# Two heads, two scan outputs and two scan directions side by side on TensorE's columns, and one modulation vector of layer 0 computed during the output projection

## The chip, the cores and the metric

The kernel runs on one core of one Trainium2 chip. The metric is the device time of one execution in microseconds (us); less is better. A core has five engines with a queue each: PE (TensorE, the matmul array), DVE (VectorE), ACT (ScalarE), POOL (GpSimd) and SP (SyncE, which here only issues DMA transfers). Each queue runs in order, and the engines wait for one another by semaphores. Matmul results land in PSUM, 128 partitions wide; everything else is held in SBUF. A matmul keeps its stationary operand (`lhsT`, up to 128 × 128) in the array and streams the moving operand (`rhs`, up to 512 columns) past it; a stationary operand with 64 or 32 columns uses that many columns of the array, and its result that many PSUM partitions.

## The reference

A block of two layers over 512 latent tokens of width 1024, with 256 context tokens in front. Layer 0 projects the normalised tokens into attention heads and a state-space scan (SSD), runs both as parallel groups of heads, and joins them in one output projection; layer 1 is a gated short convolution; each layer ends in a SwiGLU FFN. What matters here is layer 0's mixer and the modulation:

```python
mod = (silu(c) @ ada_w[i] + ada_b[i])             # six vectors of 1024
sh1, sc1, g1, sh2, sc2, g2 = split(mod, 6)
hx = rms_norm(x, norm_mix[i]) * (1 + sc1) + sh1   # sc2, sh2 for the FFN
# attention: 8 query heads of 64, 2 key/value heads, 768 keys, 512 queries
s  = q @ keys.T * 64 ** -0.5
o  = softmax(s) @ vals
# scan: 8 heads of 64, chunks of 128 tokens, two directions f and b
y_diag = ((C @ B.T) * decay) @ (x * dt)           # inside a chunk
states = B.T @ (decay_to_end * x * dt)            # what a chunk hands on
y_off  = C @ (decay * h_in)                       # from the chunks before
y = y_f + y_b + d_skip * x
x = x + g1 * (concat(o, rms_norm(y * silu(z))) @ w_out)
x = x + g2 * swiglu(rms_norm(x) * (1 + sc2) + sh2)
```

## The kernel before

All tokens are kept transposed, features on partitions and tokens on columns. Large projections split both operands in two fp32r parts, `hi` and `lo`, and run three matmuls a tile (`mm3`, L116 to L118); the splits are one ACT cast and one DVE subtraction each (`split`, L94 and L95). A weight tile of 128 × 1024 comes by DMA into one of three buffers `wst`, and is split into `whi` and `wlo` (L94, L95); `take` keeps two weights loaded ahead.

Layer 0's mixer runs after the projections of k, v, dt and q. `heads_prep` normalises the heads and applies rotary position (`rope`, L552 on; queries are written twice, L565, so that a transposed head fills 128 partitions). The context scan (`ssd_context`) and the four last feature projections follow. Then three generators are stepped in turn, in one loop at the end of `mixer`: the scan (`ssd`: eight units, each one of four chunks and one of two groups of heads, `ssd_unit`), the attention (`attention`) and the modulation of layer 0 (`ada_rest` with parts 2, 3 and 4: the mixer's gate, and the FFN's shift and scale). The Tile framework then orders each engine's instructions by data and priority, so the order in the code is only a first hint; `order` rows below show what it made.

- `ssd_states` (L645): for one chunk and group, xw (POOL, L652) times the tokens of B, whose 64 columns are held twice so that the 128 rows of the result hold both directions; of a 128-row result one direction uses 64 rows.
- `ssd_unit` (L740): decay matrices through matmuls with triangular constants (L751 to L758), exponentials on ACT, the products with dt on DVE (L768 to L774), then `yp` (L779 and L780): for two heads at once, 128 stationary columns and 2 × 128 moving ones; of the result each head takes the half of the rows that is its own, in two DVE pieces on 64 partitions (L784).
- `attn_prep` (L787): the queries of a head by four PE transposes (L791), split into q1 and q2 (L795), a first pass over the scores that finds a common shift (L802 and L804), L808.
- `attn_head` (L811): three pairs of key chunks; for each, scores (L822) into a bank psS, the exponential on ACT (L824), then the values (L830): the stationary operand has 64 columns of values and 64 of ones (`vz`), so one matmul gives the head's output in 64 rows and the softmax's sums in the other 64. Two ACT copies (L843, L844) take them out. After each second head a DVE chain turns the sums into factors (L882 to L886) and applies them (L887).
- `ada_rest` (L236): per part two accumulators of 512 columns; each takes eight DVE products (one L255, seven L257), a transpose (L260) and a reduction (L261); all parts end in one small matmul with a constant (L264) and four additions (L269).

The output projection (`project`, L897, called in `run`) sits in a block in which PE's order is that of the code: 8 output tiles d over 8 input tiles k; for the first three tiles (lead) all k but attention's last (k = 3) come first, and k = 3 last; d = 3 and 4 are whole; the last three (tail) run in two token halves. After it the FFN's norm, FFN, short convolution and second FFN follow. PSUM has eight banks: psA three of 512 columns, psV one, psS two of 1024.

## Time and profile before

| | us |
|---|---|
| median of three runs | 1294.06 (1289.82 to 1294.98) |
| the profiled execution, whole | 1294.68 |
| its span in the trace | 1292.9 |
| PE busy | 1241.5 (96%) |
| DVE busy | 731.7 (57%) |
| ACT busy | 448.0 (35%) |
| POOL busy | 182.7 (14%) |
| mean granted clock of PE | 0.989 |

Times inside the trace count from the start of the span. Busy is time in which an engine has an instruction; ends of matmuls are modelled, so that the records of neighbouring matmuls overlap and the distance between two starts is what one costs. A matmul with fp32 operands leaves two records, with half of its passes each. The granted clock of a stretch is TensorE's: 1.00 is 2.4 GHz, 0.50 is 1.2 GHz. The scan and attention lie between 144 and 331 us, the output projection's matmuls between 316 and 366.

### The profile page before, as it was taken

How to read it: one execution, taken by the hardware profiler on the slowest of the kernel's cores; microseconds unless marked ns; L12 is line 12 of the kernel's file. 1: busy time of each engine (PE TensorE's matmuls, PEld its weight loads, DVE VectorE, ACT ScalarE, POOL GpSimd, SP SyncE). 2: the span in 40 equal slices, each digit the busy share in tenths (PEclk: the TensorE clock that was granted, in tenths of full speed). 3: DMA queues.
4: the chain of work that ended last, by engine and by line, in shares of the span. 5: the costliest groups of instructions: out<-in, count | busy, mean ns of one | idle time of the engine just before them, and what ended most of it. 6: DMA issues, size and time to landing. Idle time of an engine off the chain costs nothing.

```text
span 1292.9 us, 15877 instructions
## 1 busy us (share of the span) xinstructions
PE 1241.5 (96%) x6086; PEld 1022.4 (79%) x6086; DVE 731.7 (57%) x1187; ACT 448.0 (35%) x675; POOL 182.7 (14%) x199
## 2 busy tenths in 40 slices
PE   5999988899999999999999999999999999999997
PEld 3887665567798888888888988888988888888886
DVE  4898899976464777788522564443643333332223
ACT  4534534455353222222222342223532222222221
POOL 3433435440220000000000110002200000000001
PEclk9998989999999999999999999999999999999998
DMA  9331453300413777777433323333133333333322
GB/s 370 125 98 49 123 166 119 98 1 1 149 63 122 229 250 241 226 235 255 123 102 90 115 67 97 98 98 114 50 114 98 98 98 98 92 96 90 92 88 66
DMA packets 54845, 158.52 MB, mean 123 GB/s; under 512 B 6000, under 2 KB 8688, under 8 KB 54512
## 3 DMA queue, kind: packets, MB, share of 16 engines
q1 hardware_dynamic: 54480, 157.20, 38.3%
q8 instruction: 48, 0.79, 0.3%
q10 hardware_dynamic: 288, 0.31, 0.1%
q14 instruction: 29, 0.24, 0.1%
HBM read 154.86 MB, written 2.10 MB: 121 GB/s over the span
## 4 chain that ended last, share of the span: by engine, by line
PE 83%; DVE 9%; issue 3%; DMA 3%; POOL 1%; ACT 1%; SPq 0%; DVEq 0%; ACTq 0%; POOLq 0%
PE psS L116 14%; PE psS L117 14%; PE psS L118 14%; PE psA L116 10%; PE psA L118 10%; PE psA L117 10%; PE psV L830 2%; DMA adaw<-ada 2%; PE psS L961 1%; DVE xtok L257 1%; DVE mx L804 1%; PE psS L822 1%; DVE wlo L95 1%; PE psS L963 1%; DMA xT<-xT 1%
## 5 line engine op out<-in xcount | busy, mean ns | idle before, releaser
L95 DVE TENSOR_TENSOR wlo<-wst,whi 128x1024 fp32r<-128x1024 f32 (+2 forms) x194 | 234.9, 1214 | 317.2 <-ACT whi L94 311.8
L94 ACT CAST whi<-wst 128x1024 fp32r<-128x1024 f32 (+2 forms) x194 | 198.4, 1026 | 549.9 <-PE psS L117 258.5
L116 PE MATMUL psS<-act_hi,whi 128*128 128x512 f32 x760 | 297.5, 391 | 1.0 <-DVE cs_a L573 0.9
L118 PE MATMUL psS<-act_hi,wlo 128*128 128x512 f32 x760 | 297.2, 391 | 0.0
L117 PE MATMUL psS<-act_lo,whi 128*128 128x512 f32 x760 | 297.2, 391 | 0.0
L118 PEld LDWEIGHTS psS<-act_hi,wlo 128*128 128x128 f32 x760 | 143.3, 189 | 30.0
L116 PEld LDWEIGHTS psS<-act_hi,whi 128*128 128x128 f32 x760 | 143.2, 188 | 29.3 <-issue 1.2
L117 PEld LDWEIGHTS psS<-act_lo,whi 128*128 128x128 f32 x760 | 143.2, 188 | 27.7
L325 POOL TENSOR_TENSOR sq_acc<-sq_acc,sq 128x512 f32<-128x512 f32 (+1 forms) x28 | 38.0, 1356 | 872.2 <-issue 645.7
L116 PE MATMUL psA<-ffn_h_hi,whi 128*128 128x512 f32 (+1 forms) x396 | 145.4, 367 | 0.0
L117 PE MATMUL psA<-ffn_h_lo,whi 128*128 128x512 f32 (+1 forms) x396 | 145.0, 366 | 0.0
L118 PE MATMUL psA<-ffn_h_hi,wlo 128*128 128x512 f32 (+1 forms) x396 | 145.0, 366 | 0.0
L257 DVE SCALAR_TENSOR_TENSOR ada_acc<-ada_st,silu_c,ada_acc 128x512 f32<-128x512 f32 x98 | 73.5, 750 | 25.5 <-DMA ada_st<-ada 24.0
L117 PEld LDWEIGHTS psA<-ffn_h_lo,whi 128*128 128x128 f32 x396 | 74.7, 189 | 12.0
L118 PEld LDWEIGHTS psA<-ffn_h_hi,wlo 128*128 128x128 f32 x396 | 74.7, 189 | 12.1
L116 PEld LDWEIGHTS psA<-ffn_h_hi,whi 128*128 128x128 f32 x396 | 74.7, 189 | 11.9
L116 PE MATMUL psA<-act_hi,whi 128*128 128x512 f32 (+1 forms) x216 | 80.0, 370 | 0.1
L118 PE MATMUL psA<-act_hi,wlo 128*128 128x512 f32 (+1 forms) x216 | 79.2, 367 | 0.8 <-DVE wlo L95 0.8
L117 PE MATMUL psA<-act_lo,whi 128*128 128x512 f32 (+1 forms) x216 | 79.6, 368 | 0.0
L916 DVE SCALAR_TENSOR_TENSOR xT<-psA,mod,xT 128x512 f32<-128x512 f32 (+1 forms) x40 | 25.6, 643 | 67.9 <-PE psA L118 67.7
L94 ACT CAST ffn_h_hi<-sg 128x512 fp32r<-128x512 f32 x44 | 27.3, 621 | 59.0 <-DVE sg L980 59.0
L118 PEld LDWEIGHTS psA<-act_hi,wlo 128*128 128x128 f32 x216 | 40.8, 189 | 8.1 <-DVE wlo L95 1.3
(297 smaller groups left out, 1810.7 us busy)
## 6 DMA issues: line engine op xcount, KB each, us to landing
wst<-w_gu SPq DMA_DIRECT2D x88, 512.0 KB, 3.6
ada_st<-ada SPq DMA_DIRECT2D x112, 256.0 KB, 4.0
wst<-w_dn SPq DMA_DIRECT2D x32, 512.0 KB, 3.5
wst<-ada SPq DMA_DIRECT2D x24, 512.0 KB, 3.8
wst<-w_sc SPq DMA_DIRECT2D x24, 512.0 KB, 3.7
adaw<-ada SPq DMA_DIRECT2D x16, 512.0 KB, 10.4
wst<-w_dn SPq DMA_DIRECT2D x16, 384.0 KB, 3.2
wst<-w_f SPq DMA_DIRECT2D x10, 512.0 KB, 3.6
```

Of the source, the lines that this page charges most:

```text
L94: nc.scalar.copy(hi, src)
L95: nc.vector.tensor_tensor(lo, src, hi.bitcast(F32), ALU.subtract)
L116: nc.tensor.matmul(out, lhsT=a[0], rhs=b[0], start=start, stop=False)
L117: nc.tensor.matmul(out, lhsT=a[0], rhs=b[1], start=False, stop=False)
L118: nc.tensor.matmul(out, lhsT=a[1], rhs=b[0], start=False, stop=stop)
L257: nc.vector.scalar_tensor_tensor(a, w[:, i], c, a, ALU.mult, ALU.add)
L325: nc.gpsimd.tensor_tensor(self.acc[:, ts], self.acc[:, ts], sq, ALU.add)
L804: nc.vector.tensor_reduce(mx[:, c:c + 1], s[:, 0:768], AX.X, ALU.max)
L822: nc.tensor.matmul(s[:, a * T:a * T + T], lhsT=kt[x][:, ks], rhs=q[x], start=(x == 0), stop=(x == 1))
L830: nc.tensor.matmul(av, lhsT=vz[:, kc, vs], rhs=e[:, a], start=(c + a == 0), stop=(c + a == CHUNKS - 1))
L916: nc.vector.scalar_tensor_tensor(xt[:, d, ts], ps, gate[:, d:d + 1], xt[:, d, ts], ALU.mult, ALU.add)
L961: nc.tensor.matmul(out, lhsT=a[:, k * P:(k + 1) * P], rhs=hi, start=(k == 0 and a is w[0]), stop=False)
```

## The change

**Attention.** `attn_head` becomes `attn_pair`: two heads are worked on together. The values' stationary operand is 64 columns without the ones; head 0 goes to PSUM partitions 0 to 63, head 1 to 64 to 127. The softmax's sums come from matmuls of their own with 32 columns of ones, four of them in four column groups, into a bank psA that the pair holds (`sm`). One ACT copy of 128 partitions each takes out sums and outputs. After DVE's transpose of the sums a small matmul with a new constant `pair` (L894) adds the two parts of each head; the reciprocal reads PSUM. Exponentials and queries have four buffers each instead of two. `attn_prep` makes the queries by eight matmuls of 64 columns with the identity, in place of four transposes of 128, and `rope` writes queries once.

**Scan.** B's tokens are held once. `ssd_states` runs one matmul of 64 columns for each direction, in the two column halves; `yp` runs one for each head, and one DVE piece on 128 partitions (L783) reads both.

**Modulation.** Part 4 (the FFN's scale) leaves the mixer's loop. It is queued in front of the output projection and stepped there: twice after each lead tile, three times after d = 3 and 4, and to its end before the tail. Its 512 KB loads use the `wst` buffers of the weights.

```diff
-        vz = mp.tile([P, CHUNKS, 2, 192], F32, name="vz")
-        nc.gpsimd.memset(vz, 1.0)
+        vz = mp.tile([P, CHUNKS, 2, 64], F32, name="vz")
-        qd = mp.tile([P, 4, 8, 2, 64], F32, name="qd")
+        qd = mp.tile([P, 4, 8, 64], F32, name="qd")
...
-        ada = [self.ada_rest(None, 0, (2, 3, 4), (xtok[:, 0], xtok[:, 1]))]
+        ada = [self.ada_rest(None, 0, (2, 3), (xtok[:, 0], xtok[:, 1]))]
...
+            if len(dst.shape) == 3:
+                (nc.vector, nc.gpsimd)[i].tensor_tensor(dst[:, :, o:o + 32], u, v, op)
+                continue
             for e in range(2):
                 (nc.vector, nc.gpsimd)[e].tensor_tensor(dst[:, :, e, o:o + 32], u, v, op)
...
-            nc.tensor.matmul(st[:, lo:lo + n], lhsT=sd["btok"][:, c, g].rearrange("p a b -> p (a b)"),
-                             rhs=xw.rearrange("p a b c -> p (a b c)")[:, lo:lo + n], start=True, stop=True)
+            for c, e in ends:
+                nc.tensor.matmul(st[64 * e:64 * e + 64], lhsT=sd["btok"][:, c, g], rhs=xw[:, e], start=True, stop=True)
+                out.append((g, e, st[64 * e:64 * e + 64]))
...
-            nc.tensor.matmul(yp[:, j], lhsT=xtok[:, cc, fs], rhs=mt[:, 2 * j:2 * j + 2], start=True, stop=False)
-            nc.tensor.matmul(yp[:, j], lhsT=hin[:, fs], rhs=ce[:, 2 * j:2 * j + 2], start=False, stop=True)
-            for i in range(2):
-                r = slice(64 * i, 64 * i + 64)
-                pr = 2 * g + j
-                nc.vector.scalar_tensor_tensor(y[r, pr, sl], xf[r, pr, sl], self.vec("d_skip", pr, 1)[r],
-                                               yp[r, j, i], ALU.mult, ALU.add)
+            for w, x, first in ((xtok[:, cc], mt, True), (hin, ce, False)):
+                for i in range(2):
+                    at = pr * P + 64 * i
+                    nc.tensor.matmul(yp[64 * i:64 * i + 64, j], lhsT=w[:, at:at + 64], rhs=x[:, 2 * j + i],
+                                     start=first, stop=not first)
+            nc.vector.scalar_tensor_tensor(y[:, pr, sl], xf[:, pr, sl], self.vec("d_skip", pr, 1), yp[:, j],
+                                           ALU.mult, ALU.add)
...
-            nc.tensor.transpose(out=tp[:, c], in_=qd[:, c, n].rearrange("p a b -> p (a b)"), identity=self.ident)
+            for e in range(2):
+                nc.tensor.matmul(tp[64 * e:64 * e + 64, c], lhsT=qd[:, c, n], rhs=self.ident, start=True, stop=True)
...
-    def attn_head(self, ap, q, kt, vz, u, hh):
+    def attn_pair(self, ap, qs, kt, vz, u):
+        av, sm = self.psV(), self.psA()
...
         def values(c):
-            e = es.pop(c)
+            e = [es.pop((h, c)) for h in range(2)]
+            first, last = c == 0, c == CHUNKS - 2
             for a in range(2):
                 kc = c + a + 2 if c < 4 else c + a - 4
-                nc.tensor.matmul(av, lhsT=vz[:, kc, vs], rhs=e[:, a], start=(c + a == 0), stop=(c + a == CHUNKS - 1))
+                for h in range(2):
+                    nc.tensor.matmul(av[64 * h:64 * h + 64], lhsT=vz[:, kc], rhs=e[h][:, a], start=first and a == 0,
+                                     stop=last and a == 1)
+            for h in range(2):
+                for a in range(2):
+                    r = 64 * h + 32 * a
+                    nc.tensor.matmul(sm[r:r + 32], lhsT=self.con("ones", 32), rhs=e[h][:, a], start=first, stop=last)
+        for c in range(0, CHUNKS, 2):
+            scores(0, c)
+            yield
+            scores(1, c)
+            yield
+            if c:
+                values(c - 2)
+                yield
+        values(CHUNKS - 2)
+        nc.scalar.copy(u[1], sm)
+        nc.scalar.copy(u[0], av)
...
+            nc.vector.transpose(flat, u[1])
+            tot = self.psA((P, 16))
+            nc.tensor.matmul(tot, lhsT=self.con("pair"), rhs=rt[:, :, 0], start=True, stop=True)
+            nc.vector.reciprocal(rs, tot)
...
         if lead:
             ws = [load(2 - d) for d in range(lead)]
-            part = [accumulate(d, ws[d], ks=order[:-1]) for d in range(lead)]
+            part = []
+            for d in range(lead):
+                part.append(accumulate(d, ws[d], ks=order[:-1]))
+                self.pump(2)
...
+        if lead:
+            self.pump(1000)
...
+            acc = [xp.tile([P, T], F32, name="sq", tag="sq512", bufs=2) for _ in range(2)]
+            self.queue.append(self.ada_rest(None, 0, (4,), acc))
```

The last part of attention on PE, before: L822 are scores, L830 values of one head, L116 to L118 the first matmuls of the output projection's lead.

```order
L118 MATMUL psA<-act_hi,wlo 128x512
L830 MATMUL psV<-ex,vz 128x512 x2
L822 MATMUL psS<-q_2686,kt_433 128x512
L822 MATMUL psS<-q_2687,kn_1584 128x512
L822 MATMUL psS<-q_2686,kt_433 128x512
L822 MATMUL psS<-q_2687,kn_1584 128x512
L116 MATMUL psA<-act_hi,whi 128x512
L117 MATMUL psA<-act_lo,whi 128x512
L118 MATMUL psA<-act_hi,wlo 128x512
L830 MATMUL psV<-ex,vz 128x512 x2
L116 MATMUL psA<-act_hi,whi 128x512
L117 MATMUL psA<-act_lo,whi 128x512
```

The same place on PE in the changed kernel: L832 are values (64 columns), L837 the sums (32 columns), L307 the scan's norm factors spread over partitions, L894 the fold of the sums.

```order
L822 MATMUL psS<-q_2513,kn_1575 128x512
L832 MATMUL psV<-ex,vz 64x512
L837 MATMUL psA<-ex,cons_70 32x512 x2
L298 MATMUL psA<-cons_70,sq 128x1 x7
L822 MATMUL psS<-q_2512,kt_433 128x512
L822 MATMUL psS<-q_2513,kn_1575 128x512
L822 MATMUL psS<-q_2512,kt_433 128x512
L822 MATMUL psS<-q_2513,kn_1575 128x512
L832 MATMUL psV<-ex,vz 64x512 x3
L837 MATMUL psA<-ex,cons_70 32x512 x2
```

A group of values (two heads, two key chunks) stands in two places: one matmul and the first head's sums, then, after four scores, three matmuls and the second head's sums. And the rows that end the attention there:

```order
L832 MATMUL psV<-ex,vz 64x512
L837 MATMUL psA<-ex,cons_70 32x512 x2
L832 MATMUL psV<-ex,vz 64x512 x3
L837 MATMUL psA<-ex,cons_70 32x512 x2
L307 MATMUL psA<-cons_70,rs_y 128x128 x8
L894 MATMUL psA<-rt,cons_70 128x16
L116 MATMUL psA<-act_hi,whi 128x512
L117 MATMUL psA<-act_lo,whi 128x512
L118 MATMUL psA<-act_hi,wlo 128x512
```

All lead matmuls now stand behind the last values and the fold.

DVE around the output projection's start, before: L882 to L887 turn the last heads' sums into factors, L95 is a split, L916 adds a finished output tile to the residual.

```order
L736 SCALAR_TENSOR_TENSOR yu<-xf,vecs,psA 128x512 x2
L95 TENSOR_TENSOR act_lo<-yu,act_hi 128x2x256 x2
L882 STREAM_TRANSPOSE rt<-as 128x512
L884 RECIPROCAL rs<-rt 128x16
L885 COPY rt<-rs 128x512
L886 STREAM_TRANSPOSE as<-rt 128x512
L887 TENSOR_TENSOR ao<-ao,as 128x512
L95 TENSOR_TENSOR act_lo<-ao,act_hi 128x2x256
L916 SCALAR_TENSOR_TENSOR xT<-psA,mod,xT 128x512 x2
L95 TENSOR_TENSOR wlo<-wst,whi 128x1024
```

And in the changed kernel, from the last heads' transpose (L892) on; L735 is what L736 was, L923 what L916 was:

```order
L735 SCALAR_TENSOR_TENSOR yu<-xf,vecs,psA 128x512 x2
L897 COPY rt<-rs 128x512
L255 TENSOR_SCALAR sq<-wst,silu_c 128x512
L95 TENSOR_TENSOR act_lo<-yu,act_hi 128x2x256
L898 STREAM_TRANSPOSE as<-rt 128x512
L95 TENSOR_TENSOR act_lo<-yu,act_hi 128x2x256
L257 SCALAR_TENSOR_TENSOR sq<-wst,silu_c,sq 128x512
L899 TENSOR_TENSOR ao<-ao,as 128x512
L257 SCALAR_TENSOR_TENSOR sq<-wst,silu_c,sq 128x512 x2
L95 TENSOR_TENSOR act_lo<-ao,act_hi 128x2x256
L257 SCALAR_TENSOR_TENSOR sq<-wst,silu_c,sq 128x512 x4
L260 STREAM_TRANSPOSE sq<-sq 128x512
```

The modulation's products stand between the splits of the scan's outputs, the last heads' factors and, further on, the weights' splits; all sixteen products stand ahead of the last three weights' splits. On SP the eight loads of that part (L251) stand among those of w_o: three ahead of the residual's loads, then

```order
L251 DMA wst<-ada 128x1024 x3
L108 DMA wst<-w_o 128x1024 x3
L251 DMA wst<-ada 128x1024 x2
L108 DMA wst<-w_o 128x1024 x2
L108 DMA wst<-w_gu 128x1024 x13
```

so that a weight's load waits until a modulation tile's buffer has been read.

## Rows read from the trace of the kernel before

**Rows 1.** Busy us (and instructions) of each engine by stretch, granted clock, DMA.

```profile
core 0: us, PE busy (x) PEld busy (x) DVE busy (x) ACT busy (x) POOL busy (x), PEclk, DMA share, GB/s
99.50:106.30 6.80, 5.92 (x20) 4.70 (x18) 6.80 (x11) 0.89 (x2) 4.29 (x5) 0.50 0.22 63
220.00:240.00 20.00, 15.95 (x62) 10.48 (x61) 19.73 (x33) 10.06 (x16) 10.03 (x9) 1.00 0.25 78
144.00:290.00 146.00, 127.43 (x473) 84.95 (x474) 131.80 (x213) 62.61 (x104) 74.35 (x74) 0.96 0.34 105
290.00:362.00 72.00, 70.07 (x352) 54.88 (x351) 38.95 (x63) 31.66 (x48) 8.84 (x6) 1.00 0.23 73
340.00:360.00 20.00, 19.52 (x121) 17.69 (x122) 10.95 (x12) 7.31 (x11) 8.84 (x6) 1.00 0.52 158
```

**Rows 2.** DVE from 144 to 290, costliest groups: count, busy us, mean ns, idle.

```profile
L257 DVE SCALAR_TENSOR_TENSOR xtok<-wst,silu_c,xtok 128x512 f32<-128x512 f32 x42 | 40.6, 967 | 1.1 <-DMA wst<-ada 0.4
...
L784 DVE SCALAR_TENSOR_TENSOR xf<-xf,vecs,psA 64x128 f32<-64x128 f32 x26 | 8.9, 343 | 8.1 <-PE psA L780 7.9
...
L260 DVE STREAM_TRANSPOSE xtok<-xtok 128x512 f32<-128x512 f32 x6 | 4.2, 705 | 0.1
L261 DVE TENSOR_REDUCE ada_red<-xtok 128x16 f32<-128x512 f32 x6 | 4.1, 677 | 0.1
L255 DVE TENSOR_SCALAR xtok<-wst,silu_c 128x512 f32<-128x512 f32 x6 | 3.2, 532 | 0.5 <-POOL xw L652 0.5
```

**Rows 3.** PE, groups of the whole trace: values, and the states' two shapes.

```profile
L830 PE MATMUL psV<-ex,vz 128*128 128x512 f32 x96 | 46.8, 611 | 0.0
...
L656 PE MATMUL psA<-xw,btok 128*128 128x256 f32 x24 | 8.1, 447 | 0.9 <-DVE zf L479 0.5 <-POOL xw L652 0.4
...
L656 PE MATMUL psA<-xw,btok 128*128 128x512 f32 x8 | 4.5, 641 | 2.8 <-POOL xw L652 1.8 <-ACT btok L590 1.0
```

**Rows 4.** Chain of waits: 150 to 290 by line; after 290, start, us, pieces.

```profile
by line: DVE xtok L257 12.5%; DVE mx L804 8.8%; issue 7.5%; PE psV L830 7.3%; DVE lx L773 4.2%; DVE xf L784 3.2%; PE psS L822 3.1%; PE psA L656 3.1%; DVE ce L768 2.6%; DMA wst<-ada 2.6%; DMA wst<-w_o 2.6%; PE psA L779 2.5%; PE psS L757 2.5%
...
297.07 0.44 PE psA L791 x4
...
297.94 0.43 PE psA L780 x2
...
298.38 1.72 PE psV L830 x4
...
311.52 1.78 PE psA L307 x16
...
317.11 0.23 PE psA L118
```

**Rows 5.** PE, order of time: start, us, records, around one strip group.

```profile
39.36 0.53 PE L118 MATMUL psA<-whi,act_lo 128*128 128x272 f32 x3
39.82 0.64 PE L203 MATMUL psS<-adaw,silu_w 128*32 128x256 f32 x8
40.39 0.40 PE L118 MATMUL psV<-whi,act_lo 128*128 128x272 f32 x1
```

**Rows 6.** Rope's query writes on DVE and POOL; PE, first wait for DVE.

```profile
L565 DVE TENSOR_TENSOR qd<-rp_u,rp_v 128x256 f32<-128x256 f32 x8 | 4.3, 564 | 0.0
...
L565 POOL TENSOR_TENSOR qd<-rp_u,rp_v 128x256 f32<-128x256 f32 x8 | 7.8, 990 | 1.8 <-DVE rp_v L561 1.8
...
99.08 0.81 PE L584 MATMUL psA<-cons,xf 128*128 128x128 f32 x4 [2.22 <-DVE xf L576]
```

**Rows 7.** Start of the output projection in order of time: DVE, PE.

```profile
312.45 1.41 DVE L736 SCALAR_TENSOR_TENSOR yu<-xf,vecs,psA 128x512 f32<-128x512 f32 x2 [1.38 <-PE psA L307]
...
331.17 0.71 DVE L882 STREAM_TRANSPOSE rt<-as 128x512 f32<-128x512 f32 x1 [11.34 <-ACT as L843]
...
339.21 1.22 DVE L95 TENSOR_TENSOR wlo<-wst,whi 128x1024 fp32r<-128x1024 f32 x1
...
340.48 0.50 PE L118 MATMUL psA<-act_hi,wlo 128*128 128x512 f32 x1 [0.84 <-DVE wlo L95]
```

More of the change, by code (lines that the diff above doesn't have):

```diff
@@ L587, in to_tok @@
         else:
-            s = tp.rearrange("p c (g n) -> p c g n", g=2)
-            for c in range(nc_):
-                nc.scalar.copy(btok[:, c0 + c], s[:, c, :, None, :].broadcast_to([P, 2, 2, 64]))
+            nc.scalar.copy(btok[:, c0:c0 + nc_], tp.rearrange("p c (g n) -> p c g n", g=2))
     def ssd_decay(self, mp, dt, sd):
@@ L852, in attention, with prep, advance @@
                                  self.con("ones")[64:128, None, :].broadcast_to([64, 6, P]), AF.Copy, scale=-1.0 / 64)
-        prep = lambda n: self.attn_prep(ap, qd, kt[n // 4][0], n, ones)
-        p = prep(0)
-        q = next(p)
-        next(p)
-        next(p)
+        def prep(n):
+            return self.attn_prep(ap, qd, kt[n // 4][0], n, ones)
+        def advance(steps):
+            for _ in range(steps):
+                while nxt and next(nxt[0], 1) is not None:
+                    nxt.pop(0)
@@ L858, in attention, with begin @@
+        def begin(p):
+            gens = [prep(2 * p + h) for h in range(2)]
+            return gens, [next(g) for g in gens]
+        nxt, qs = begin(0)
+        advance(4)
         yield
[L859 to L862 removed]
+        advance(4)
         yield
[L864 to L894 removed]
@@ new lines, in attention @@
+        advance(4)
+        for p in range(4):
+            u = [ap.tile([P, T], F32, name=x, tag=x, bufs=1) for x in ("ao", "as")]
+            pair = self.attn_pair(ap, qs, kt[p // 2], vz[:, :, p // 2], u)
+            next(pair)
+            if p < 3:
+                nxt, qn = begin(p + 1)
+            for x in range(4):
+                next(pair, None)
+                advance(1)
+                next(pair, None)
+                advance(2)
+                if x < 3:
+                    yield
+            advance(10)
+            rt = ap.tile([P, 16, 32], F32, name="rt", tag="rt", bufs=1)
+            flat = rt.rearrange("p a b -> p (a b)")
+            nc.vector.transpose(flat, u[1])
+            tot = self.psA((P, 16))
+            nc.tensor.matmul(tot, lhsT=self.con("pair"), rhs=rt[:, :, 0], start=True, stop=True)
+            rs = ap.tile([P, 16], F32, name="rs", tag="rs", bufs=1)
+            nc.vector.reciprocal(rs, tot)
+            nc.vector.tensor_copy(rt, rs[:, :, None].broadcast_to([P, 16, 32]))
+            nc.vector.transpose(u[1], flat)
+            nc.vector.tensor_tensor(u[0], u[0], u[1], ALU.mult)
+            self.split(*m.at(p), halves(u[0]))
+            qs = qn
```

96 lines of the change are left out of this document (22 added, 74 removed).

## The prediction

> **What bounds the kernel now.** I read first the busy time by stretch, then the costliest groups of the stretch that the change touches, then the chain of waits inside it. From 144 to 290 us (scan units, features and attention together) VectorE is busy 131.80 of 146 us and TensorE 127.43; between 220 and 240 VectorE has 19.73 of 20 and TensorE 15.95. From 290 to 362 TensorE has 70.07 of 72 and VectorE 38.95 [rows 1]. So VectorE bounds the first stretch, with 146 − 127.43 = 18.6 us in which TensorE stands, and TensorE the second. The chain agrees: from 150 to 290 its largest line is the modulation product L257, 12.5% of 140 us, 17.5 us; after 290 it runs through matmuls back to back [rows 4]. All that follows the output projection is TensorE at work on code that does not change, so a gain or loss ahead of it reaches the end as it is.
>
> **The change, part by part.**
>
> *VectorE loses work before 290.* One of three modulation parts leaves: 14 L257 of 967 ns (42 stand there for three parts), 2 L255 of 532, 2 L260 of 705, 2 L261 of 677 [rows 2]: 13.5 + 1.1 + 1.4 + 1.4 = 17.4 us. The scan outputs' accumulation goes from 32 pieces on 64 partitions at 343 ns [rows 2] to 16 on 128; taken at the same 343 each, 16 × 0.343 = 5.5 us go, of which about 5 lie here. Together 22.5 us. Lower bound of its worth: what the chain holds, a third of L257's 17.5 us (5.8) and half of L784's 3.2% (2.2), so 8. Upper bound: 22.5, if nothing else is late next. I take 15: VectorE has almost no idle time where this work stands, but TensorE can draw closer by its 18.6 us of standing at most, and next in line stand the waits between PE, ACT and VectorE of each scan unit, which stay. **−15 (−8 to −22.5).**
>
> *Queries' preparation.* Rope writes each query half once, not twice: 4 VectorE writes of 564 ns and 4 GpSimd writes of 990 go, where TensorE stood 2.22 us for VectorE at 99.08 [rows 6]. 2.3 us leave VectorE's queue ahead of that gap; I take −1.5. Behind the gap the granted clock is 0.50 until 106.3 [rows 1], the lower level (1.2 GHz); if a shorter gap left it at 2.4 GHz a further 3.4 would go: **−1.5 (0 to −5).**
>
> *Columns TensorE streams.* A piece of fp32 matmul with 512 columns takes 1.72/4 = 0.43 us and two such pieces are one matmul, 0.86; with 256 columns 0.43 [rows 4].
> - Values. 48 matmuls of 0.86 (96 pieces [rows 3], of which 64 lie before 290) are 41.2 us. Now each of twelve groups (a pair of heads, two key chunks) has 4 matmuls in 64 columns and 4 sums in 32 columns. Were all side by side, a group would take 2 × 0.86 + 0.86 = 2.6 against 3.43: −10.3 in all. But TensorE's order keeps the halves apart: one matmul and two sums of the first head, all in the left half (1.7 us), other work, then the rest (2.6). That is 4.3 a group, **+10.3** at the worst. Some groups have their sums together or their pieces next to each other; I take **+6.8**.
> - Scan outputs: 32 matmuls of 0.43 become 64 of 0.215 in pairs: 13.7 to 6.9, **−6.9**. States (24 + 8 pieces [rows 3]): 12 × 0.43 + 4 × 0.86 = 8.6 becomes 20 × 0.43 in pairs, 4.3: **−4.3**. Query transposes: 0.44 for four [rows 4], 32 in all, 3.5 us; as 64 matmuls of 0.215 in pairs 6.9: **+3.4**. The four new fold matmuls: +0.4.
> Sum −0.6 (−17.7 to +2.9). That column tiles do run side by side, the trace shows: eight pieces of the 32-column strips at 39.82, 0.2 us each were they one after another, have the next matmul start 0.57 us later [rows 5].
>
> *Changing between array shapes.* The order has some 88 changes between whole and halved array that before lacks. The one place where before shows it is that strip group: three 272-column pieces start at 39.36 and the group 0.46 later where 3 × 0.13 were due, and the way out costs as much: about 0.1 us each [rows 5]. 88 × 0.1 = 8.8; before 290, where TensorE stands 18.6 us anyway, most of it is hidden: **+4.4 (0 to +12).** The Trainium skill, "TensorEngine Tiling (Array Packing)", Key Properties, says that a change of tiling mode drains the engine. It gives no price; by it all 88 would stand on the path, and the sum would be 4.4 worse.
>
> *The output projection.* Before, TensorE's lead rows stand between the last heads' values; now all of them stand behind L307 and the new fold L894. Count from the last sums. (1) VectorE has two L735 (1.41 [rows 7]) ahead of the transpose L892 (0.71), begun once half of L307's 1.78 us [rows 4] is through: L894 can start near 3.1, TensorE is there at 1.8: 1.4 late. VectorE's queue then holds 0.5 to 0.7 us pieces: two splits, two L735, the copy, L255, and only then the third and fourth scan splits (7.8 and 9.2), for which TensorE, after 15 matmuls of 0.23 [rows 4] on what is ready, asks at 6.8 and, three matmuls on, at 8.5: 1.0 + 0.7 more. Together 3. (2) d=3's wlo (1.22 us) stands behind 27 pieces of about 0.7, some 20 us, so ready at 23 to 25, while TensorE wants it at 22; before it waits 0.84 [rows 7]: +1.5. (3) The moved part's fold L264 stands behind d=4 in TensorE's order; by then VectorE has 9.5 us more to do and TensorE 10.9: +0.5. The eight 512 KB loads go through the weights' ring; the tile that frees it for d=3 is read about when (2) counts, so no term of their own. VectorE has the room: 10.95 of 20 us busy between 340 and 360 [rows 1]. **+5 (0 to +12).** The dropped memset and ACT's fewer copies are off the path: nothing, unless GpSimd or ACT became late there.
>
> Sum: −15 − 1.5 − 0.6 + 4.4 + 5 = −7.7. The profiled run took 1294.68 us (span 1292.9), the median is 1294.06: 1287.0 and 1286.4. I say 1287.
>
> **The rivals.**
> - *The relief counts whole.* TensorE follows VectorE all the way, the pieces of a group fall next to each other and run side by side: values at half their +6.8: −22.5 − 1.5 − 4 + 4.4 + 5 = −18.6, **1276**. For it: 99% busy VectorE in the very stretch where the part stood, four buffers of exponentials for two. Against: the order with the pieces apart.
> - *TensorE takes over.* Every change of shape costs its 0.1, the split values their 10.3, and the relief is cut to 12: −12 − 1.5 + 2.9 + 8.8 + 5 = +3.2, **1297**: no change that shows. For it: TensorE was already busy 87% there.
> - *Slower: VectorE becomes the bound of the output projection.* The moved part puts 14 L257 into VectorE's queue ahead of d=3's and d=4's wlo. If each costs the 967 ns [rows 2] instead of 0.7 and the loads in the shared ring (a weight waits for a modulation tile to be read) put d=3 and d=4 each 4 us later, that stage costs 14, not 5. It decides once the relief is under 10: −8 − 1.5 − 0.6 + 4.4 + 14 = +8.3, **1302**.
>
> **How the numbers follow.** Forecast 0.40 (own range 1281 to 1293), whole relief 0.23, TensorE takes over 0.21, slower 0.16. The range 1272 to 1301 spans the first three and cuts the first's far end and half of the last. A measurement tells apart some 0.5%, 6.5 us. Faster by more (under 1287.6): over half of the forecast and the whole second case, 0.24 + 0.23 = 0.47; within: 0.32; slower (over 1300.5): 0.21.
>
> **What would show it.** VectorE busy some 22 us less from the start of the scan to the end of attention, and the last head's copy (before, its DVE transpose starts at 331.17 [rows 7]) some 10 to 14 us earlier while no L257 of that part stands before it. Column pieces of one head's values next to each other with starts 0.43 apart rather than shared: the split; shared starts across both halves: the second case. TensorE waiting at L894, at the third and fourth scan operands and at d=3's wlo, about 5 us in sum: step (1) to (3); 10 or more: the slower case. It is wrong altogether if the scan's stretch does not shrink though VectorE has less to do, which would mean that its waits and not its work set it.

## The result

The changed kernel takes 1325.58 us (median of four runs, 1324.82 to 1329.86), the kernel before 1294.47 beside it; the ratio is 1.0255, 95% interval 1.0223 to 1.0288. It is slower by some 31 us, where 1287 was forecast and the range ended at 1301. The profiled execution took 1324.94 us with a span of 1323.1.

The same view of the changed kernel as [rows 1], busy time by stretch, from the start of the scan to the end of attention and for the output projection:

```profile
core 0: us, PE busy (x) PEld busy (x) DVE busy (x) ACT busy (x) POOL busy (x), PEclk, DMA share, GB/s
144.00:336.50 192.50, 174.78 (x857) 93.72 (x856) 128.39 (x204) 73.16 (x118) 63.08 (x65) 0.94 0.17 54
160.00:180.00 20.00, 12.98 (x59) 8.34 (x59) 19.05 (x28) 6.82 (x13) 5.51 (x8) 0.57 0.50 165
220.00:240.00 20.00, 19.48 (x129) 11.76 (x129) 13.10 (x26) 8.68 (x14) 9.54 (x10) 1.00 0.00 1
340.00:360.00 20.00, 16.92 (x73) 12.99 (x71) 15.51 (x26) 3.45 (x5) 0.00 (x0) 1.00 0.69 233
360.00:380.00 20.00, 14.05 (x43) 10.98 (x43) 12.97 (x19) 5.98 (x7) 4.46 (x3) 0.74 0.65 213
```

Two stretches of the kernel before that [rows 1] does not have, in the same columns:

```profile
144.00:330.60 186.60, 166.94 (x646) 113.01 (x647) 153.80 (x255) 82.43 (x136) 74.35 (x74) 0.97 0.27 82
160.00:180.00 20.00, 16.25 (x57) 11.57 (x56) 18.04 (x27) 6.72 (x12) 7.25 (x11) 0.83 0.53 160
```

From 144 on the last values and sums now end at 335.9 (ACT's copy of the sums starts there), against 330.6 before, although 34 of the output projection's 63 lead matmuls, 34 × 0.23 = 7.8 us, and L307 (1.78 [rows 4]) had been done by then before, and are not now. So scan and attention themselves take some 15 us more, not 11 less. VectorE is indeed relieved: 128.39 us in 192.5, before 153.80 in 186.6, and 13.10 of 20 between 220 and 240 where before it had 19.73 [rows 1]. TensorE is busy 19.48 of those 20. But over the whole stretch it stands nearly as long as before, 192.5 − 174.78 = 17.7 us against 186.6 − 166.94 = 19.7: from 160 to 180 it stands 7 us, before 3.75, and its granted clock there is 0.57, before 0.83. After the values the FFN's norm begins (its first matmul, L333) at 391.8 where before it began at 361.5: 56 us against 31, 25 more: 7.8 for the lead matmuls and 2 for L307, which have only moved behind the values, 9 for waits (below), and some 5 for the clock, whose 0.74 from 360 to 380 is 10.4 us at the lower level. PE is busy 16.92 of 20 us from 340 to 360 and 14.05 from 360 to 380. That it all lies ahead of that point shows in the ends: L333 is 30.3 us later, the span 30.2 longer.

How a group of values looks now, on PE in order of time (start, us, records; two records are one matmul); L832 are values in 64 columns, L837 sums in 32:

```profile
330.99 1.07 PE L832 MATMUL psV<-ex,vz 128*64 128x512 f32 x2
331.99 1.05 PE L837 MATMUL psA<-ex,cons 128*32 128x512 f32 x4
332.98 1.93 PE L832 MATMUL psV<-ex,vz 128*64 128x512 f32 x6
334.84 1.05 PE L837 MATMUL psA<-ex,cons 128*32 128x512 f32 x4
```

One matmul of the first head takes 1.00 (330.99 to 331.99), its two sums, side by side, 0.99, then three matmuls 1.86 and two sums 0.98: 4.83 us. (In three of the twelve groups the first sums come together with later ones, which saves about 1 us each.) Before, a group took 2 × 1.72 = 3.44 [rows 4]. In the three, second and first head run side by side and the last stands alone. The passes alone, ten at 0.43, would be 4.30; the four changes between 64 and 32 columns add the other 0.53, some 0.13 each; nothing of the second head runs beside the first head's sums, although its columns are free.

PE's waits after the values (the wait is in brackets, with what ended it):

```profile
339.10 0.40 PE L894 MATMUL psA<-rt,cons 128*128 128x16 f32 x2 [1.23 <-DVE rt L892]
...
359.35 0.50 PE L116 MATMUL psA<-act_hi,whi 128*128 128x512 f32 x1 [2.84 <-ACT whi L94]
...
361.30 0.80 PE L118 MATMUL psA<-act_hi,wlo 128*128 128x512 f32 x1 [1.21 <-DVE wlo L95]
...
374.03 0.64 PE L264 MATMUL psA<-ada_red,cons 128*128 128x32 f32 x2 [4.74 <-DVE ada_red L261]
```

1.23 + 2.84 + 1.21 + 4.74 = 10.0 us, before 0.84 [rows 7]. What stands behind the second and third is seen on VectorE and on SP's queue:

```profile
347.37 1.53 DVE L257 SCALAR_TENSOR_TENSOR sq<-wst,silu_c,sq 128x512 f32<-128x512 f32 x2
353.15 1.54 DVE L257 SCALAR_TENSOR_TENSOR sq<-wst,silu_c,sq 128x512 f32<-128x512 f32 x2 [4.25 <-DMA wst<-ada]
...
341.71 3.65 SPq L1053 DMA_DIRECT2D xT<-xT  x8
345.46 3.80 SPq L251 DMA_DIRECT2D wst<-ada  x3
354.72 5.74 SPq L108 DMA_DIRECT2D wst<-w_o  x3
```

VectorE waits 4.25 us for modulation tiles; SP issues the second three of them only at 345.46, behind the residual's eight loads, and the next weights of w_o at 354.72, when the modulation tiles in the ring (the three buffers `wst`) have been read.

### The profile page after: what moved, and what is told of

The parts are those of the page before. It is cut to its first block, busy times and chain, and to the rows that moved or that the text cites. A ratio compares the mean times of both kernels' runs of the same rounds, so it can differ in the third digit from the quotient of the medians.

```text
span 1323.1 us, 16337 instructions
## 1 busy us (share of the span) xinstructions
PE 1263.7 (96%) x6360; PEld 1013.8 (77%) x6360; DVE 720.5 (54%) x1171; ACT 443.3 (34%) x663; POOL 168.6 (13%) x194
## 4 chain that ended last, share of the span: by engine, by line
PE 84%; DVE 9%; issue 3%; DMA 2%; ACT 1%; POOL 1%; SPq 0%; DVEq 0%; POOLq 0%; ACTq 0%
PE psS L116 14%; PE psS L117 14%; PE psS L118 14%; PE psA L118 10%; PE psA L116 10%; PE psA L117 10%; PE psV L832 2%; PE psA L837 1%; PE psS L973 1%; PE psS L822 1%; DVE xtok L257 1%; DVE wlo L95 1%; DMA wst<-ada 1%; DVE lx L772 1%; PE psS L203 1%
## 5 line engine op out<-in xcount | busy, mean ns | idle before, releaser
L95 DVE TENSOR_TENSOR wlo<-wst,whi 128x1024 fp32r<-128x1024 f32 (+2 forms) x194 | 232.8, 1203 | 311.3 <-ACT whi L94 306.5
L116 PE MATMUL psS<-act_hi,whi 128*128 128x512 f32 x760 | 296.5, 390 | 0.8 <-DVE cs_a L575 0.7
L118 PE MATMUL psS<-act_hi,wlo 128*128 128x512 f32 x760 | 296.1, 390 | 0.0
L118 PEld LDWEIGHTS psS<-act_hi,wlo 128*128 128x128 f32 x760 | 142.8, 188 | 29.9
L116 PEld LDWEIGHTS psS<-act_hi,whi 128*128 128x128 f32 x760 | 142.7, 188 | 29.0 <-issue 0.9
L116 PE MATMUL psA<-ffn_h_hi,whi 128*128 128x512 f32 (+1 forms) x396 | 145.2, 367 | 0.0
L118 PE MATMUL psA<-ffn_h_hi,wlo 128*128 128x512 f32 (+1 forms) x396 | 144.7, 365 | 0.0
L257 DVE SCALAR_TENSOR_TENSOR ada_acc<-ada_st,silu_c,ada_acc 128x512 f32<-128x512 f32 x98 | 73.4, 749 | 24.4 <-DMA ada_st<-ada 22.7
L116 PE MATMUL psA<-act_hi,whi 128*128 128x512 f32 (+1 forms) x216 | 81.3, 377 | 2.8 <-ACT whi L94 2.8
L118 PEld LDWEIGHTS psA<-ffn_h_hi,wlo 128*128 128x128 f32 x396 | 74.7, 189 | 12.1
L116 PEld LDWEIGHTS psA<-ffn_h_hi,whi 128*128 128x128 f32 x396 | 74.7, 189 | 11.9
L118 PE MATMUL psA<-act_hi,wlo 128*128 128x512 f32 (+1 forms) x216 | 80.9, 375 | 1.2 <-DVE wlo L95 1.2
L923 DVE SCALAR_TENSOR_TENSOR xT<-psA,mod,xT 128x512 f32<-128x512 f32 (+1 forms) x40 | 25.6, 643 | 70.6 <-PE psA L118 70.5
L116 PEld LDWEIGHTS psA<-act_hi,whi 128*128 128x128 f32 x216 | 41.9, 194 | 10.5 <-ACT whi L94 3.3
L118 PEld LDWEIGHTS psA<-act_hi,wlo 128*128 128x128 f32 x216 | 41.7, 193 | 8.5 <-DVE wlo L95 1.6
## 6 DMA issues: line engine op xcount, KB each, us to landing
adaw<-ada SPq DMA_DIRECT2D x16, 512.0 KB, 10.4
```

What stands on the lines that cost most here:

```text
L95: nc.vector.tensor_tensor(lo, src, hi.bitcast(F32), ALU.subtract)
L116: nc.tensor.matmul(out, lhsT=a[0], rhs=b[0], start=start, stop=False)
L118: nc.tensor.matmul(out, lhsT=a[1], rhs=b[0], start=False, stop=stop)
L257: nc.vector.scalar_tensor_tensor(a, w[:, i], c, a, ALU.mult, ALU.add)
L923: nc.vector.scalar_tensor_tensor(xt[:, d, ts], ps, gate[:, d:d + 1], xt[:, d, ts], ALU.mult, ALU.add)
```

## The experiments

Each was timed against the kernel before on the same chip: e and h on one (1293.72 and 1293.79 us for the kernel before), f on a second (1292.93), g on a third (1294.29), so that a difference between medians of two chips is known to 1 or 2 us. Theory A: the heads are the main loss. Theory B: the moved modulation part is. The table has, from each profiled execution, the starts of the first and the last value matmul, how many lead matmuls stand before the last, and the start of L333 (the FFN norm's first matmul, whatever its line in that run); then the median and the ratio with its interval.

| kernel | values | lead before | L333 | median | ratio |
|---|---|---|---|---|---|
| before | 175.4 to 329.9 | 34 | 361.5 | 1294.47 | |
| after | 181.5 to 334.3 | 0 | 391.8 | 1325.58 | 1.0255 (1.0223 to 1.0288) |
| e1 modulation alone | 173.2 to 320.2 | 34 | 372.7 | 1304.95 | 1.0096 (1.0069 to 1.0123) |
| e2 all but modulation | 181.5 to 336.6 | 0 | 380.7 | 1315.27 | 1.0178 (1.0156 to 1.0199) |
| e3 scan alone | 174.4 to 321.7 | 34 | 353.2 | 1285.69 | 0.9946 (0.9928 to 0.9964) |
| e4 scan and modulation | 174.7 to 315.5 | 34 | 367.0 | 1301.10 | 1.0066 (1.0047 to 1.0085) |
| f1 e3, part 4 behind second pair | 174.1 to 322.3 | 34 | 353.9 | 1286.83 | 0.9951 (0.9935 to 0.9968) |
| f2 e3, part 4 behind third pair | 174.3 to 311.2 | 0 | 354.3 | 1287.94 | 0.9958 (0.9938 to 0.9977) |
| f3 e1 without the loads | 175.0 to 320.3 | 34 | 365.4 | 1298.77 | 1.0039 (1.0027 to 1.0052) |
| g1 e1, fold later | 173.7 to 320.6 | 34 | 364.7 | 1298.12 | 1.0030 (1.0013 to 1.0047) |
| f4 e2, values together | 190.3 to 322.5 | 0 | 367.0 | 1300.14 | 1.0054 (1.0035 to 1.0074) |
| g3 f4, modulation later | 182.9 to 319.2 | 0 | 363.6 | 1297.33 | 1.0028 (1.0018 to 1.0038) |
| g4 e3 and queries | 170.3 to 319.6 | 34 | 351.2 | 1284.45 | 0.9924 (0.9910 to 0.9939) |
| h1 f4, scan first, fold's bank | 196.3 to 328.6 | 18 | 365.2 | 1299.09 | 1.0050 (1.0034 to 1.0066) |
| h2 f4, scan first | 196.6 to 327.1 | 0 | 369.3 | 1308.15 | 1.0111 (1.0081 to 1.0142) |

**The change taken apart.** e1 is the kernel before with the modulation's hunks of the diff, e2 the changed kernel without them, e3 the kernel before with the scan's hunks (`ssd_states`, `ssd_unit` and what feeds them), e4 both e1's and e3's edits.

```diff
e1
-        ada = [self.ada_rest(None, 0, (2, 3, 4), (xtok[:, 0], xtok[:, 1]))]
+        ada = [self.ada_rest(None, 0, (2, 3), (xtok[:, 0], xtok[:, 1]))]
...
+            self.queue.append(self.ada_rest(None, 0, (4,), acc))
...
e3
-            nc.tensor.matmul(yp[:, j], lhsT=xtok[:, cc, fs], rhs=mt[:, 2 * j:2 * j + 2], start=True, stop=False)
...
+                    nc.tensor.matmul(yp[64 * i:64 * i + 64, j], lhsT=w[:, at:at + 64], rhs=x[:, 2 * j + i],
+                                     start=first, stop=not first)
...
```

> The kernel before with one part of the change: the FFN's scale vector (modulation part 4) is computed during the output projection; attention and scan stay as they were. Theory A (the pairing of the heads is the main loss, because a group of values comes in two places and because the lead matmuls no longer stand between the values): this part takes 17 us from VectorE before 290 and puts some 9 us of waits on TensorE in the output projection, so 1288 to 1296. Theory B (the moved part is the main loss: loads in the shared ring and VectorE's queue): 1308 or more.

> The changed kernel with the modulation's part 4 put back beside scan and attention; heads, scan outputs and directions stay side by side. Theory A: most of the loss stays, 1312 to 1322. Theory B: at or under the kernel before, 1285 to 1300.

> The kernel before with the scan's part alone: scan outputs and directions side by side (64-column matmuls, one VectorE piece for two heads); heads one after another as before, modulation as before. Theory A: TensorE streams 11 us less and VectorE 5 less, minus some 40 changes of array shape at 0.1 us, so 1284 to 1294. Theory C (every change of array shape stands on the path and eats what the columns save): 1294 to 1302.

> The changed kernel with attention as before (one head after another, ones beside the values, queries by transposes): the scan's part and the moved modulation part together. Theory A: 1280 to 1292, the lead matmuls stand between the values again. Theory B: 1305 or more.

The scan's part gains 8 us, as theory A has it. The moved modulation part costs 11 us alone and 1301.10 − 1285.69 = 15 beside the scan's; that is more than theory A gave it and less than theory B. The heads, with the queries' preparation (which costs nothing by itself, g4 below), cost 1315.27 − 1285.69 = 30 us: theory A. The sum −8 + 30 + 1325.58 − 1315.27 = −8 + 30 + 10 = 32 is the loss. e1 shows both sides of its part: the last values come 9.7 us earlier, and from there to L333 it takes 52.5 us in place of 31.6. VectorE and PE of e1 in the output projection:

```profile
320.81 0.48 DVE L255 TENSOR_SCALAR sq<-wst,silu_c 128x512 f32<-128x512 f32 x1 [10.73 <-PE psV L830]
...
340.08 0.79 PE L116 MATMUL psA<-act_hi,whi 128*128 128x512 f32 x1 [9.56 <-ACT whi L94]
...
353.77 0.64 PE L264 MATMUL psA<-ada_red,cons 128*128 128x32 f32 x2 [5.01 <-DVE ada_red L261]
```

The first product (L255) does not read what L830 writes, yet VectorE waits 10.73 us for the last L830: its target (`sq`) must lie where attention's buffers were. Until the last values are done three modulation tiles hold the ring of three weight buffers, and d = 3's weight comes 9.56 us late. At the fold PE waits 5.01 more. Behind both waits the granted clock is low (columns as above):

```profile
340.00:348.80 8.80, 8.65 (x24) 6.11 (x24) 6.00 (x7) 2.11 (x3) 0.00 (x0) 0.66 0.76 248
353.00:362.00 9.00, 8.23 (x25) 6.66 (x26) 3.26 (x8) 2.21 (x3) 4.26 (x3) 0.64 0.43 141
```

0.66 over 8.8 us and 0.64 over 9.0 are 6.0 and 6.5 us at the lower level, some 3 us lost each. 9.6 + 5.0 + 3 + 3 = 20.6 of the 20.9 us.

**Loads or VectorE?** f3 keeps e1's sixteen products but leaves out their loads; g1 keeps both and issues the fold later (and two steps of the part, not three, after d = 3 and 4).

```diff
f3
-                            nc.vector.scalar_tensor_tensor(a, w[:, i], c, a, ALU.mult, ALU.add)
+                            nc.vector.scalar_tensor_tensor(a, w[:, i] if w is not None else self.stand, c, a,
+                                                           ALU.mult, ALU.add)
g1
-            self.pump(3)
-        if lead:
-            self.pump(1000)
+            self.pump(2)
         ws = [load(2 + more - i) for i in range(tail)]
         for e in range(2):
             for i, d in enumerate(range(KC - tail, KC)):
                 terms = accumulate(d, ws[i], e)
+            if lead:
+                self.pump(1000)
```

> The kernel e1_mod_only, but the moved part's eight loads are left out: its sixteen products read a tile of attention's result in their place, so the scale vector is a wrong one and the sixteen products cost the same. Theory D (the loads are the cost: three modulation tiles sit in the ring of weight buffers until attention's space is free for their sums, so the weight of d=3 comes late, 9.6 us, and the next modulation tiles come late too, 5.0 us at the fold): the waits at d=3 and at the fold go, 1284 to 1291. Theory E (VectorE's queue is the cost: the products stand ahead of the weights' splits): within 4 us of e1, 1301 to 1308.

> The kernel e1_mod_only, with the moved part's last step (its fold on TensorE and the steps ahead of it) issued after the first half of the tail instead of ahead of the tail. Theory J (TensorE's fixed order makes the whole tail wait for VectorE at the fold, 5.0 us, and the granted clock drops behind the wait): 1296 to 1300. If the wait only goes elsewhere (to the tail's weights, which stand behind the same products): 1302 to 1307.

PE's waits in f3 at d = 3 and at the fold (L266 there):

```profile
333.39 0.50 PE L118 MATMUL psA<-act_hi,wlo 128*128 128x512 f32 x1 [1.00 <-DVE wlo L95]
...
346.79 0.63 PE L266 MATMUL psA<-ada_red,cons 128*128 128x32 f32 x2 [8.12 <-DVE ada_red L263]
```

and in g1:

```profile
339.68 0.79 PE L116 MATMUL psA<-act_hi,whi 128*128 128x512 f32 x1 [8.70 <-ACT whi L94]
...
353.93 0.41 PE L264 MATMUL psA<-ada_red,cons 128*128 128x32 f32 x2 [1.05 <-DVE ada_red L261]
```

Without the loads the wait at d = 3 goes from 9.56 to 1.00, so the loads in the ring are its cause; but TensorE reaches the fold that much earlier and waits 8.12 there in place of 5.01. The gain is 6 us and 1298.77 lies between the two theories' ranges, less than theory D said, since the rest of the cost moves to the next place in TensorE's fixed order. With the fold later (g1) that wait is 1.05 and the gain 7 us, as theory J said. So both theories hold a part: the loads hold up d = 3, the products' late start holds up the fold.

**VectorE's relief without the output projection's cost.** f1 and f2 keep part 4 in the mixer but put its first instruction behind a later one.

```diff
-                nc.vector.transpose(flat, u[1])
+                x = nc.vector.transpose(flat, u[1])
+                if n == 3:
+                    self.mark = x.ins
...
+        self.pump(1000, [self.ada_rest(None, 0, (4,), (xtok[:, 0], xtok[:, 1]), behind=self.mark)])
```

(f2: `n == 5`.)

> Scan side by side as in e3, heads as before; the modulation's part 4 stays in the mixer (sums in the context's token tiles, which are free from the start of attention), but its first VectorE instruction stands behind the transpose that ends the second pair of heads, some 260 us in, where VectorE has room. If the relief that e1 showed before the end of attention (the last values 9.7 us earlier than in the kernel before) comes from VectorE's work alone, this keeps it without the cost in the output projection: 1275 to 1281. If the work then stands in the way of the last scan units: 1283 to 1288.

> As f1, but behind the transpose that ends the third pair of heads, where the scan is over: 1275 to 1281 if VectorE's work is what counts; 1285 or more if the part then meets the output projection's weights in the shared ring of buffers.

Neither gains over e3 (1285.69). In f2 the last values are 10.4 us earlier, as in e1, but the lead matmuls then stand behind them, and L333 is no earlier. So the 9.7 us of e1 are not a gain that one has only to keep: what attention gives back, the stretch behind it takes. Both runs miss the 1275 to 1281 that relief alone would have given.

**The heads.** f4 fixes the order of a group on PE; no wait is added, only an order on the engine.

```diff
-                for h in range(2):
-                    nc.tensor.matmul(av[64 * h:64 * h + 64], lhsT=vz[:, kc], rhs=e[h][:, a], start=first and a == 0,
-                                     stop=last and a == 1)
+                for h in (1, 0):
+                    run(nc.tensor.matmul(av[64 * h:64 * h + 64], lhsT=vz[:, kc], rhs=e[h][:, a], start=first and a == 0,
+                                         stop=last and a == 1))
...
+            def run(x):
+                if prev:
+                    self.tc.add_manual_dep(x.ins, prev[-1].name, info, reason="group")
+                prev.append(x.ins)
```

> The kernel e2_no_mod, with the order inside each group of values fixed: four value matmuls, second head first and heads in turn, then the four sums. Theory F (the heads' loss is that a group comes in two places): the group goes from 4.8 us to 2.8, twelve times, 24 us, of which what TensorE's bound stretch shows: 1291 to 1300. Theory G (changes of array shape and the lead matmuls behind the attention are the loss): 1306 to 1316.

The last two groups of f4 on PE (values L840, sums L845):

```profile
318.31 1.94 PE L840 MATMUL psV<-ex,vz 128*64 128x512 f32 x8
320.18 1.07 PE L845 MATMUL psA<-ex,cons 128*32 128x512 f32 x8
321.17 1.94 PE L840 MATMUL psV<-ex,vz 128*64 128x512 f32 x8
323.04 1.07 PE L845 MATMUL psA<-ex,cons 128*32 128x512 f32 x8
```

A group takes 1.87 + 0.99 = 2.86 us, from 4.83: 12 × 1.97, less 3 for the three groups named above, is some 21 us of TensorE's time, of which 1315.27 − 1300.14 = 15 show. So the group in two places is half of the heads' loss. The time lies at the upper end of theory F's range and under theory G's, and the other half, some 14 us against e3, is left. The two traces show where on TensorE it lies. From 144 to L333 it is busy 197.5 of 223.0 us in f4 and 192.5 of 209.2 in e3: 9 us more standing, and 5 us more work, while the clock is at the lower level for some 17 us longer. Most of both lies from 160 to 180, here e3 and then f4:

```profile
160.00:180.00 20.00, 17.85 (x74) 11.67 (x73) 19.35 (x29) 5.97 (x12) 9.43 (x14) 0.91 0.51 159
160.00:180.00 20.00, 12.35 (x49) 7.87 (x51) 19.45 (x27) 6.67 (x14) 5.51 (x8) 0.57 0.50 162
```

TensorE stands 7.65 us there in place of 2.15, with VectorE busy nearly all the time in both, and the clock is 0.57 in place of 0.91. Three more runs looked for what makes it so.

```diff
g3
-            if rounds:
+            if rounds >= 3:
                 self.pump(3, ada)
h1, h2
-            alive = (next(a, 1) is None) or alive
+            alive = (rounds >= 3 and next(a, 1) is None) or alive or rounds < 3
h1
-            tot = self.psA((P, 16))
+            tot = self.psS()[:, 0:16]
```

(g3 has also the order of the products behind the second head's preparation.)

> The kernel f4_values_together, with the modulation's products beginning only behind the second head's preparation (NoSync order on VectorE), not beside the preparation of the first two heads. Theory H (two heads are prepared before the first values, in a stretch that VectorE bounds, so TensorE starves there, at 0.57 of its clock from 160 to 180, and values and scan start 15 us later): first values at 180 or earlier instead of 190, 1286 to 1295. Theory I (what is left of the loss is the lead matmuls behind attention): first values earlier or not, 1298 to 1303.

> The kernel f4_values_together with two more edits: the attention is first stepped in the fourth round, so that the scan's first unit is issued ahead of the first two heads' preparation, and the fold of the sums (L894) writes into a psS bank, not a psA bank. Theory K (the lead matmuls wait behind the attention because their psA banks come after the fold's, and because the scan ends late): some 20 or more of the 63 lead matmuls stand before the last values again, 1284 to 1292. If TensorE was not the bound at the attention's end, the lead's place changes nothing: 1296 to 1301.

> As h1, but the fold stays in a psA bank; so the scan is first, and the lead matmuls stay behind the attention. Theory K: the part of the gain that comes from the bank is missing, 1290 to 1298 and slower than h1 by 3 to 8. If the scan's place does it all: as h1.

In g3 the first values come at 182.9 instead of 190.3, and the total gains 3 us of the 7. Its stretches show why (columns as above): VectorE has hardly any room from 160 to 260, so what is put off early stands in the way later.

```profile
160.00:180.00 20.00, 16.86 (x89) 10.76 (x89) 18.78 (x29) 7.78 (x16) 10.08 (x15) 0.83 0.33 102
180.00:200.00 20.00, 18.09 (x87) 8.37 (x85) 19.59 (x29) 7.65 (x13) 3.34 (x4) 1.00 0.48 158
220.00:240.00 20.00, 15.99 (x91) 8.82 (x90) 19.96 (x34) 7.36 (x14) 6.30 (x6) 1.00 0.37 113
240.00:260.00 20.00, 16.94 (x92) 9.22 (x91) 19.89 (x29) 9.31 (x15) 13.95 (x11) 1.00 0.47 148
```

TensorE stands 3.1 us from 160 to 180, no longer 7.65, but more than in f4 behind that. So theory H is near on the start (it said 180) and wrong on the price (1297.33, where it said 1295 at most). In h1 the lead matmuls stand between the last values again:

```profile
321.46 1.94 PE L840 MATMUL psV<-ex,vz 128*64 128x512 f32 x8
323.33 1.07 PE L845 MATMUL psA<-ex,cons 128*32 128x512 f32 x8
324.33 0.50 PE L116 MATMUL psA<-act_hi,whi 128*128 128x512 f32 x1
...
327.27 1.94 PE L840 MATMUL psV<-ex,vz 128*64 128x512 f32 x8
```

18 of them, with the fold's bank as the only difference to h2, where there are none; and h1 is faster than h2, by 9 us in the medians and by 4 in the profiled executions (1298.85 and 1302.94; h2's four lie between that and 1311.29). That part of theory K is shown: with the scan first, the fold's PSUM bank, which is given out ahead of the lead's, keeps the lead behind the attention. Its prices are not: h1 and h2 both lie above the ranges it gave, and h1 lies where it should be if the lead's place changed nothing. The scan put first takes back what the bank gives (h2 stands 2 us behind f4 by the profiled executions, 8 by the medians), so h1 stands where f4 stood. So it is seen where the rest of the heads' loss, some 14 us against e3, lies: TensorE stands and its clock falls, above all from 160 to 180. What causes it is not settled: two heads' preparation ahead of the first values and the lead's place each have a hand in it, and no run took both away.

**The queries.** g4 adds to e3 the single rope write and the identity matmuls.

```diff
-            nc.tensor.transpose(out=tp[:, c], in_=qd[:, c, n].rearrange("p a b -> p (a b)"), identity=self.ident)
+            for e in range(2):
+                nc.tensor.matmul(tp[64 * e:64 * e + 64, c], lhsT=qd[:, c, n], rhs=self.ident, start=True, stop=True)
```

> The kernel e3_scan_only, with the queries' preparation of the change added: rope writes each query once, and eight identity matmuls of 64 columns take the place of four transposes. By the prediction's terms −1.5 for rope and +3.4 for the streams, partly hidden: 1284 to 1289 (against 1285.7 of e3). If the shape changes and streams of the 64 matmuls all stand on the path: 1290 to 1294.

1284.45 us, ratio 0.9924 (0.9910 to 0.9939): the scan's and the queries' parts of the change together make the fastest kernel of the study, 10 us under the kernel before. That the queries' part adds to the scan's is likely and not shown: the intervals of g4 and e3 overlap, and they ran on two chips.

## Why the prediction was wrong

- **What bounds the kernel** was read right, and used wrongly. VectorE bounded the stretch to 260 us, and taking work from it brought the last values 9.7 us forward (e1) where 15 was taken; within the bounds of 8 to 22.5. But the relief was to draw on TensorE's 18.6 us of standing, and half of the changes of shape were to hide in the same time: two terms counted on it. And the relief did not last beside the other parts: it moves the last values by 6 us beside the scan's (e4 against e3, from the table) and by 2.3 beside the heads (the changed kernel against e2). TensorE's standing hardly went, 17.7 us where it was 19.7, since it stands 7 us from 160 to 180 where it stood 3.75. The prediction's own sign of being wrong altogether, that the stretch does not shrink though VectorE has less to do, came true in the changed kernel; in e1, with the heads one after another, the stretch did shrink, so there VectorE's work had set it.
- **The heads** are where the forecast failed most. The terms for values, queries and fold come to +9.1 (6.8 − 1.5 + 3.4 + 0.4), to +13.5 even with all that was taken for changes of shape, and the heads cost 30. *Streams:* the order showed the two places, and 4.3 us a group was the worst end. The passes of a group took just that, and with 3 us less for three groups they cost 12 × (4.30 − 3.44) − 3 = some 7 more, where 6.8 was taken; the changes between sums and values, 0.53 a group, come on top and make it 12 × 1.39 − 3 = some 14. f4, which undoes it and more, gives 15 us back. That the size of the passes was right is in part luck: pieces next to each other were to save something, and where they did stand so (330.99 to 335.8), it did not help, because sums and values have different column widths and do not run beside each other. *Standing:* the other 14 us (f4 less e3), 9 of standing and the rest at the lower clock, above all from 160 to 180, had no term.
- **Changes of shape** at 0.1 us each were near (0.13). The Trainium skill, "TensorEngine Tiling (Array Packing)", Key Properties, says that a change of tiling mode drains TensorE; the trace agrees as far as it goes, since the four changes of the group above lengthen it by 0.53 us. That half of them would be hidden is a step that failed: of the 21 us of TensorE's time that f4 takes out of the groups of values, changes included, 15 show in the total, over two thirds.
- **Scan outputs and states** (−6.9, −4.3, and 5 us of VectorE's) were right in kind and too large: −8.0 as a whole (e3), its changes of shape included. **Queries**: predicted −1.5 and +3.4 on the two engines; g4 is 1 us (medians) to 3 us (ratios) faster than e3. What was hoped for ahead of the scan came in full: the wait of 2.22 us at 99.08 is gone in the changed kernel and in g4, and the clock from 99.5 to 106.3 is 1.00 in place of 0.50 in both; little of it is left in g4's total.
- **The output projection**: +5 was taken; 25 came in the changed kernel, 15 of them without the lead matmuls and L307, and 21 in e1. Step (1), at L894 and the scan's operands, was near: 1.23 + 0.24 us of waits where 3 was taken. Steps (2) and (3), 1.5 and 0.5, measure 2.84 + 1.21 and 4.74 in the changed kernel, 9.56 and 5.01 in e1. The sentence that failed is that the loads in the ring have no term of their own: I counted VectorE's instructions from the last values on, and not that the sums' tiles lie in space that attention frees only then, with three tiles held in the ring all that time and the next three behind the residual's loads on SP. One term was missing: the clock after each wait, some 5 us in the changed kernel and some 3 us for each wait in e1. The lead matmuls, 7.8 us, which I called moved, only changed sides; what their place costs is the 4 to 9 us between h2 and h1.
- **The rivals.** The slower one named the right place, and its price of 14 for that stage was near the 15. Of its two halves the loads in the ring came; the slower products did not (1.53 us for two L257, not 967 ns each). The case in which TensorE takes over had every change of shape and the split values at their full price, which is what the streams showed. Neither had the heads' standing, and no case let the paired heads cost 30, so all were too low, and a chance of 0.21 for slower was too small for a change that rearranged the order of four engines.

## What to carry to other kernels

Two stationary halves save columns only if both halves' instructions stand next to each other in the engine's order with the same tile shape; look for that in the order before counting the saving, and fix it there where the scheduler separates them. Work that is moved to a stretch where its engine has room also takes its buffers along: ask where its result lies and from when that space is free, what its loads hold while they wait, and what stands behind it in a fixed order. Terms that hide in the same idle time are to be counted once.
